# A two-layer retention and RG-LRU trunk on one core: every engine in the order of the program, weights split in two parts, first squares, softplus and final scaling regrouped

## The chip, the cores and the metric

The kernel runs on one core of one Trainium2 chip. The metric is the device time of one execution in microseconds (us); of the kernel before there are three runs, and their median counts.

## What is computed

The input x has 256 tokens of 2048 features, in float32. Two layers follow each other, and in each

- h = rmsnorm(x) g1, and one projection p = h w_in of width 6144, split into q, k, v, g of 1024 each (eight retention heads of 128) and xb, yb of 1024 each (the recurrent branch);
- retention per head: q and k are rotated, the scores are multiplied by a decay matrix, the weighted v is normalised over the head (mean and variance) and multiplied by silu(g);
- the recurrent branch: a causal convolution of 4 taps over xb, two gates (small block-diagonal products), a = exp(-8 r softplus(-lambda)), a linear recurrence over the tokens (a scan), times gelu(yb), and an rmsnorm over the branch;
- x = x + [retention, recurrent] w_out, then the feed-forward x = x + (silu(h w_gate) * (h w_up)) w_down with h = rmsnorm(x) g2 and 5632 inner features.

A last rmsnorm with its own gain gives the output. All products are made in float32 quality: an operand is the exact sum of two parts, and three of the four products of parts are taken.

## The kernel before, in words

Features lie on the 128 partitions and tokens along the free axis, so x is 16 chunks of [128 x 256]. A weight of 128 output features and up to 2048 inputs is one unit (a slot of 1 MB). For each unit SP loads `raw` (`load`, L533, three buffers), ACT copies it to its high part `whi` (L557), DVE subtracts to get the low part `wlo` (L558), and PE makes 16 pairs of products: the high weight with both parts of the operand (512 columns, L193) and the low weight with the high operand (256 columns, L195). Four pairs are a block, four blocks a unit. The first eight units of a layer make v with the roles exchanged (L438 to L440: three products of 512 columns per piece and half of the tokens, 24 in a unit). `split(n + 2, part)` (L549) runs while unit n is multiplied, in three parts, in front of blocks 0, 1 and 2; behind the last part the load of unit n + 5 is issued. The first four units of layer 0 come in quarters, together with quarters of x; `pair` (L122) makes the two parts of an operand: ACT the high (L126, L129), DVE the low (L127, L130).

Everything small follows the stream of blocks by a count of ticks, one for each block (`Ticks`, L51): `tk.after(n, f)` writes the instructions of f n blocks later. The head's scores (L237) come 5 ticks after k is done, the decayed scores (DVE, L244) 1 tick later, the weighted product (PE, L251) 2 ticks after that, the moments (DVE and POOL, L261 to L265) 1, the normed head (DVE, L272) 2, its transposes (PE, L286) 2, the gated mix and its pair 1. The recurrent branch goes from the convolution (ACT L317, DVE L319) over the gates (PE, L328) to tanh, exp and square on ACT (L336 to L340), square roots (L353), the scan (DVE, L360) and the accumulated squares (ACT L169, DVE L170). `sums` (L136) makes the norm's columns on PE (L141) and the power on POOL (L145); `spread` (L148) makes a row of them on all partitions, with a diagonal made by DVE (L153) and a product with ones (L155). After the recurrent branch's norm, eight ticks in a row each write a mix (L393) and its pair.

The program's order is not the order of the queues: the scheduler of the tile framework orders the instructions of each engine when the program is closed, and gives out buffers.

At the start POOL squares and adds the 16 chunks of x (L607 to L611), the sums follow at tick 23, their row at tick 25, and `softplus` (L565, 30 small operations on DVE) is written at tick 29. Eight small products warm PE up (L592). At the end the last chunk's square goes through `sums` together with the accumulated ones, `spread` makes the row, ACT copies it (L636), and 16 scalings of one chunk each follow (12 on DVE, L642; 4 on POOL, L640), with a transfer after every two, from SP and ACT in turn (L643).

Of the kernel before, what the change touches and what calls it, by code (L numbers as in the profile page):

```python
# [16 lines left out]
P = 128  # L17
T = 256
# [10 lines left out]
WARM = 8  # L29
# [21 lines left out]
class Ticks:  # L51
    """Work that follows the stream of large products, some ticks behind."""
# [18 lines left out]
class Unit:  # L71
    """One slot of a weight: its source, its width, its products, what follows."""

    def __init__(self, src, width, blocks, done=None, begin=None):
        self.src, self.width, self.blocks = src, width, blocks
        self.done, self.begin = done, begin
        self.split_at = (0, 1, 2)
# [3 lines left out]
def trunk(ctx: ExitStack, tc, a, out):  # L81
    nc = tc.nc
    pool = lambda name, bufs, **k: ctx.enter_context(tc.tile_pool(name=name, bufs=bufs, **k))
# [20 lines left out]
    # ---- constants and parameters  # L104
# [31 lines left out]
    def sums(parts, n, key):  # L136
        """1 / sqrt(sum over partitions and parts / n + eps), a column for each half of the tokens."""
        ps = small()
        for j in range(2):
            for i, x in enumerate(parts):  # L140
                PE.matmul(ps[:, j : j + 1], lhsT=x[:, j * P : (j + 1) * P], rhs=ones[:, 0:1],  # L141
                          start=i == 0, stop=i == len(parts) - 1)
        rc = two_p.tile([P, 2], F32, tag="rc", name="rc")
        V.tensor_scalar(out=rc, in0=ps[:, 0:2], scalar1=1.0 / n, scalar2=EPS, op0=ALU.mult, op1=ALU.add)  # L144
# [27 lines left out]
    def joined_halves(ps):  # L172
        """The two halves of a sum of products, added."""
# [5 lines left out]
    def column_unit(src, n_k, operand, done, begin=None, order=None):  # L179
        """128 output features, all tokens: n_k pieces of the contraction."""  # L180
# [22 lines left out]
    # ---- retention  # L203
# [10 lines left out]
    def head(l, h):  # L214
        c = {}

        def g_done(ps):
            """2 silu(g) = g (1 + tanh(g / 2))"""
# [81 lines left out]
    # ---- recurrent branch  # L300
    def lru(l, n):
# [30 lines left out]
        def decays():  # L332
            """r, i = (1 + tanh(./2)) / 2;  log a = n4sp (1 + tanh);  1 - a^2 = -tanh(log a) (1 + a^2)"""
# [45 lines left out]
        def cubic():  # L379
            """2 gelu(y) = y (1 + tanh(GELU (y + 0.044715 y^3)))"""  # L380
# [20 lines left out]
    # ---- norms between the blocks  # L401
# [4 lines left out]
    def after_residual(k, nxt, gains):  # L406
        """Chunk k of the residual is new: its part of the next norm and operand."""
# [12 lines left out]
    def v_units(l):  # L420
        """All tokens of half of v, 4 pieces of the contraction to a slot."""
# [38 lines left out]
    def layer_units(l):  # L460
# [15 lines left out]
        # output projection; the last head is the last to be ready  # L476
        order = [0, 1, 2, 3, 4, 5, 6] + list(range(8, 16)) + [7]
        for n in range(KD):
# [7 lines left out]
            if n == 1:  # L486
# [4 lines left out]
                u.split_at = (4, 4, 4)  # L491
            res.append(u)

        # feed-forward
# [26 lines left out]

    def last(k):
        if k < KD - 1:
            accumulate("xa", X[:, k, :], k == 0)
        else:
# [23 lines left out]
    def split(n, part, parts=3):  # L549
# [15 lines left out]
    def softplus():  # L565
        """-4 softplus(-lam), with log1p(e) = 2 artanh(e / (2 + e))"""
        lam = par[:, i0 : i0 + nl]
        V.tensor_scalar(out=sp[0], in0=lam, scalar1=-1.0, scalar2=None, op0=ALU.mult)
        V.tensor_tensor(out=sp[1], in0=sp[0], in1=lam, op=ALU.max)
        S.activation(out=sp[1], in_=sp[1], func=AF.Exp, scale=-1.0)  # L570
        V.tensor_scalar(out=sp[2], in0=sp[1], scalar1=2.0, scalar2=None, op0=ALU.add)
        V.reciprocal(out=sp[2], in_=sp[2])
        V.tensor_tensor(out=sp[1], in0=sp[1], in1=sp[2], op=ALU.mult)
# [141 lines left out]
```

## Time and profile before

| | |
|---|---|
| median of three runs | 2266.14 us (2265.61 to 2266.22) |
| span of the profiled execution, first to last instruction | 2262.9 us |
| mean granted TensorE clock | 0.996 |
| PE busy | 2239.7 us (99%) |
| DVE busy | 1530.3 us (68%) |
| ACT busy | 1160.7 us (51%) |
| POOL busy | 85.3 us (4%) |
| read from memory | 418.77 MB, 186 GB/s over the span |

The span leaves out what lies before the first and after the last instruction of the program; no time of its own is given for the profiled execution beside the span, which is 3.2 us below the median of the runs. Busy time is the union of an engine's instructions; PE's matmuls are pipelined and their ends are modelled. A row of a wait names the engine and line that waited, and the one that ended the wait. The lines are those of the kernel before.

### The profile page before, as it was taken

What the parts mean: (1) busy time and instruction counts of PE and PEld (TensorE: products, weight loads), DVE (VectorE), ACT (ScalarE), POOL (GpSimd) and SP (SyncE); (2) the same over time, 40 slices, a digit from 0 to 9 for tenths busy, and PEclk for the clock granted to TensorE, in tenths of its full rate; (3) what the DMA queues carried; (4) which work ended last, traced back from release to release, by engine and by line L of the source; (5) the groups of instructions that cost most, each with busy time, mean ns of one, the idle gap of its engine ahead of it and who ended that gap; (6) DMA issues with size and microseconds to landing.
All of it is one profiled execution on the core that took longest, in us unless ns stands there. A gap on an engine that the chain in (4) does not pass through costs nothing.

```text
span 2262.9 us, 32580 instructions
## 1 busy us (share of the span) xinstructions
PE 2239.7 (99%) x12748; PEld 1949.9 (86%) x12748; DVE 1530.3 (68%) x2818; ACT 1160.7 (51%) x2040; POOL 85.3 (4%) x128
## 2 busy tenths in 40 slices
PE   8999999999999999999999999999999999999997
PEld 6888888888888888888888888888888888888886
DVE  8788877666566666666758889776665666566665
ACT  5666644555344543445546765455543455444553
POOL 4001110000000000000000101000000000000000
PEclk9999999999999999999999999999999999999999
DMA  7455455555555555555555554555555555555553
GB/s 254 176 177 197 179 177 186 187 192 192 188 189 189 192 185 198 186 189 184 191 200 179 180 192 168 180 186 188 195 184 194 187 190 192 185 196 186 189 182 114
DMA packets 63721, 422.96 MB, mean 187 GB/s; under 512 B 7376, under 2 KB 8016, under 8 KB 25168
## 3 DMA queue, kind: packets, MB, share of 16 engines
q1 hardware_dynamic: 61200, 414.60, 51.7%
q0 software_dynamic: 1792, 5.24, 0.8%
q8 instruction: 99, 1.62, 0.3%
q10 hardware_dynamic: 576, 1.05, 0.1%
q14 instruction: 54, 0.44, 0.1%
HBM read 418.77 MB, written 2.10 MB: 186 GB/s over the span
## 4 chain that ended last, share of the span: by engine, by line
PE 97%; DVE 1%; DMA 1%; issue 0%; POOL 0%; ACT 0%; SPq 0%; DVEq 0%; POOLq 0%
PE acc_ps L193 61%; PE acc_ps L195 31%; PE v_ps L439 1%; PE v_ps L438 1%; PE v_ps L440 1%; PE sm_ps L328 1%; DVE wlo L558 1%; DMA x<-in_x_dram 0%; PE sm_ps L237 0%; DVE op L130 0%; DMA raw<-in_w_v_dram 0%; PE sm_ps L155 0%; PE sm_ps L286 0%; DVE x L642 0%; PE sm_ps L238 0%
## 5 line engine op out<-in xcount | busy, mean ns | idle before, releaser
L193 PE MATMUL acc_ps<-op,whi 128*128 128x512 f32 x6016 | 2105.6, 396 | 0.0
L195 PE MATMUL acc_ps<-op,wlo 128*128 128x256 f32 x6016 | 1672.9, 278 | 0.0
L193 PEld LDWEIGHTS acc_ps<-op,whi 128*128 128x128 f32 x6016 | 1128.8, 188 | 263.3
L558 DVE TENSOR_TENSOR wlo<-raw,whi 128x683 fp32r<-128x683 f32 (+5 forms) x1204 | 1007.5, 851 | 458.4 <-ACT whi L557 457.4
L557 ACT ACTIVATE whi<-raw 128x683 fp32r<-128x683 f32 (+5 forms) x1204 | 860.8, 754 | 853.3 <-PE acc_ps L193 765.7
L195 PEld LDWEIGHTS acc_ps<-op,wlo 128*128 128x128 f32 x6016 | 1131.5, 188 | 0.7
L403 DVE TENSOR_TENSOR x<-acc_ps,x 128x256 f32<-128x256 f32 x128 | 54.3, 424 | 219.1 <-PE acc_ps L195 219.1
L176 DVE TENSOR_TENSOR z<-acc_ps,low 128x256 f32<-128x256 f32 x256 | 107.1, 419 | 2.2 <-ACT low L175 2.2
L175 ACT ACTIVATE low<-acc_ps 128x256 f32<-128x256 f32 x256 | 93.9, 367 | 9.2 <-PE acc_ps L195 9.2
L126 ACT ACTIVATE op<-mix 128x256 fp32r<-128x256 f32 x104 | 43.4, 417 | 71.9 <-DVE mix L507 68.9
L502 ACT ACTIVATE sg<-z 128x256 f32<-128x256 f32 x88 | 36.8, 418 | 67.5 <-DVE z L501 67.5
L145 POOL TENSOR_TENSOR rc<-rc,mhalf 128x2 f32<-128x2 f32 x7 | 7.7, 1096 | 1684.8 <-DVE rc L144 1684.8
L439 PE MATMUL v_ps<-wlo,op 128*128 128x512 f32 x128 | 52.3, 409 | 7.5 <-DVE wlo L558 7.5
L404 DVE TENSOR_TENSOR x<-acc_ps,x 128x256 f32<-128x256 f32 x128 | 54.3, 424 | 4.3
L438 PE MATMUL v_ps<-whi,op 128*128 128x512 f32 x128 | 51.6, 407 | 1.2 <-ACT op L129 1.2
L440 PE MATMUL v_ps<-whi,op 128*128 128x512 f32 x128 | 51.7, 404 | 0.1
L127 DVE TENSOR_TENSOR op<-mix,op 128x256 fp32r<-128x256 f32 x104 | 43.5, 419 | 0.2
L439 PEld LDWEIGHTS v_ps<-wlo,op 128*128 128x128 f32 x128 | 25.3, 197 | 15.0 <-DVE wlo L558 10.1
L506 DVE TENSOR_TENSOR sg<-sg,rs 128x256 f32<-128x256 f32 x88 | 36.9, 420 | 0.8 <-ACT sg L502 0.8
L507 DVE TENSOR_TENSOR mix<-z,sg 128x256 f32<-128x256 f32 x88 | 36.9, 419 | 0.0
L501 DVE TENSOR_TENSOR z<-z,rs 128x256 f32<-128x256 f32 x88 | 36.9, 419 | 0.0
L130 DVE SCALAR_TENSOR_TENSOR op<-x,par,op 128x256 fp32r<-128x256 f32 x64 | 34.3, 539 | 0.2 <-ACT op L129 0.2
(114 smaller groups left out, 729.5 us busy)
## 6 DMA issues: line engine op xcount, KB each, us to landing
raw<-in_w_gate_dram SPq DMA_DIRECT2D x88, 1024.0 KB, 4.8
raw<-in_w_up_dram SPq DMA_DIRECT2D x88, 1024.0 KB, 4.8
raw<-in_w_in_dram SPq DMA_DIRECT2D x80, 1024.0 KB, 4.8
raw<-in_w_down_dram SPq DMA_DIRECT2D x64, 960.0 KB, 4.7
raw<-in_w_out_dram SPq DMA_DIRECT2D x32, 1024.0 KB, 4.8
raw<-in_w_down_dram SPq DMA_DIRECT2D x32, 896.0 KB, 4.5
raw<-in_w_v_dram SPq DMA_DIRECT2D x12, 1024.0 KB, 4.7
raw<-in_w_v_dram SPq DMA_DIRECT2D x16, 256.0 KB, 6.5
```

Of the source, the lines that this page charges most:

```text
L127: V.tensor_tensor(out=t[:, 1, :], in0=x_ap, in1=t[:, 0, :].bitcast(F32), op=ALU.subtract)
L175: S.activation(out=low, in_=ps[:, T : 2 * T], func=AF.Copy)
L176: V.tensor_tensor(out=z, in0=ps[:, 0:T], in1=low, op=ALU.add)
L193: PE.matmul(u.ps, lhsT=u.hi[:, w], rhs=x2.rearrange("p a t -> p (a t)"), start=k == order[0], stop=False)
L195: PE.matmul(u.ps[:, T : 2 * T], lhsT=u.lo[:, w], rhs=x2[:, 0, :], start=False, stop=k == order[-1])
L403: V.tensor_tensor(out=X[:, k, :], in0=ps[:, T : 2 * T], in1=X[:, k, :], op=ALU.add)
L404: V.tensor_tensor(out=X[:, k, :], in0=ps[:, 0:T], in1=X[:, k, :], op=ALU.add)
L438: PE.matmul(ps, lhsT=x2[:, 0, t], rhs=u.hi[:, w], start=k == 0, stop=False)
L439: PE.matmul(ps, lhsT=x2[:, 0, t], rhs=u.lo[:, w], start=False, stop=False)
L440: PE.matmul(ps, lhsT=x2[:, 1, t], rhs=u.hi[:, w], start=False, stop=k == KD - 1)
L557: S.activation(out=u.hi[:, w], in_=u.raw[:, w], func=AF.Copy)
L558: V.tensor_tensor(out=u.lo[:, w], in0=u.raw[:, w], in1=u.hi[:, w].bitcast(F32), op=ALU.subtract)
```

## The change

All engines take their instructions in the order in which the program writes them. A weight is split in two parts (of up to 1024 columns), in front of blocks 0 and 2. Twelve products warm up in place of eight. The first squares are made by ACT, four chunks at a time, at ticks 14 to 17, into a tile of the tag that v takes later (one buffer), and folded by DVE one tick later into a tile with two rows of tokens; the sums come at tick 20 and their row at tick 22. Softplus is written in six pieces at ticks 29 to 34. `spread` takes the column itself, broadcast, as the stationary operand and the identity as the moving one. Before the end the accumulated squares are summed early, the last chunk's square is added to them, and the scalings are four on DVE with three chunks each and four on POOL, with four transfers of four chunks.

```diff
-WARM = 8
+WARM = 12
 class Unit:
-        self.split_at = (0, 1, 2)
+        self.split_at = (0, 2)
 def trunk(ctx: ExitStack, tc, a, out):
     nc = tc.nc
+    ctx.enter_context(tc.manual_schedule())
...
     def sums(parts, n, key):
...
+        inverse_root([ps[:, 0:2]], n, key)
+
+    def inverse_root(columns, n, key):
         rc = two_p.tile([P, 2], F32, tag="rc", name="rc")
-        V.tensor_scalar(out=rc, in0=ps[:, 0:2], scalar1=1.0 / n, scalar2=EPS, op0=ALU.mult, op1=ALU.add)
+        w = 2 // len(columns)
+        for j, c in enumerate(columns):
+            V.tensor_scalar(out=rc[:, j * w : (j + 1) * w], in0=c, scalar1=1.0 / n, scalar2=EPS, op0=ALU.mult, op1=ALU.add)
         G.tensor_tensor(out=rc, in0=rc, in1=mhalf, op=ALU.pow)
...
     def spread(key):
-        dg = one_p.tile([P, 2, P], F32, tag="dg", name="dg")
         ps = small()
         for j in range(2):
-            V.tensor_scalar(out=dg[:, j, :], in0=ident, scalar1=st[key + "c"][:, j : j + 1], scalar2=None, op0=ALU.mult)
-        for j in range(2):
-            PE.matmul(ps[:, j * P : (j + 1) * P], lhsT=ones, rhs=dg[:, j, :], start=True, stop=True)
+            PE.matmul(ps[:, j * P : (j + 1) * P], lhsT=st[key + "c"][:, j : j + 1].to_broadcast([P, P]), rhs=ident,
+                      start=True, stop=True)
...
+    def last_sums():
+        st["last_ps"] = [small(), small()]
+        for j in range(2):
+            PE.matmul(st["last_ps"][j][:, 0:1], lhsT=st["xa"][:, j * P : (j + 1) * P], rhs=ones[:, 0:1], start=True, stop=False)
     def last(k):
         if k < KD - 1:
             accumulate("xa", X[:, k, :], k == 0)
+            if k == KD - 2:
+                tk.after(3, last_sums)
...
-    def split(n, part, parts=3):
+    def split(n, part, parts=2):
...
-    xa = one_p.tile([P, T], F32, tag="acc", name="acc")
-    G.tensor_tensor(out=xa, in0=X[:, 0, :], in1=X[:, 0, :], op=ALU.mult)
-    for k in range(1, KD):
-        sq = tmp("sq")
-        G.tensor_tensor(out=sq, in0=X[:, k, :], in1=X[:, k, :], op=ALU.mult)
-        G.tensor_tensor(out=xa, in0=xa, in1=sq, op=ALU.add)
-    tk.after(23, lambda: sums([xa], D, "rs"))
-    tk.after(25, lambda: rows("rs"))
-    tk.after(29, softplus)
+    def squares(i):
+        sq = one_p.tile([P, 4, T], F32, tag="v", name="sq4")
+        S.activation(out=sq, in_=X[:, 4 * i : 4 * i + 4, :], func=AF.Square)
+        tk.after(1, lambda: folded(i, sq))
+    def folded(i, sq):
+        if i == 0:
+            st["xa2"] = one_p.tile([P, 2, T], F32, tag="rotl", name="acc2")
+            V.tensor_tensor(out=st["xa2"], in0=sq[:, 0:2, :], in1=sq[:, 2:4, :], op=ALU.add)
+        else:
+            V.tensor_tensor(out=sq[:, 0:2, :], in0=sq[:, 0:2, :], in1=sq[:, 2:4, :], op=ALU.add)
+            V.tensor_tensor(out=st["xa2"], in0=st["xa2"], in1=sq[:, 0:2, :], op=ALU.add)
+    for i in range(4):
+        tk.after(14 + i, lambda i=i: squares(i))
+    tk.after(20, lambda: sums([st["xa2"][:, 0, :], st["xa2"][:, 1, :]], D, "rs"))
+    tk.after(22, lambda: rows("rs"))
+    for i, part in enumerate(softplus()):
+        tk.after(29 + i, part)
...
-                for part in range(3):
+                for part in range(2):
...
-    sums([st["xa"], st["sq"]], D, "rs")
+    for j in range(2):
+        PE.matmul(st["last_ps"][j][:, 0:1], lhsT=st["sq"][:, j * P : (j + 1) * P], rhs=ones[:, 0:1], start=False, stop=True)
+    inverse_root([ps[:, 0:1] for ps in st["last_ps"]], D, "rs")
...
-    for k in range(0, KD, 2):
-        for j in (k, k + 1):
-            if j % 4 == 3:
-                G.tensor_tensor(out=X[:, j, :], in0=X[:, j, :], in1=rs, op=ALU.mult)
-            else:
-                V.tensor_tensor(out=X[:, j, :], in0=X[:, j, :], in1=ps, op=ALU.mult)
-        (nc.sync if k % 4 == 0 else S).dma_start(out=out[:, k : k + 2], in_=X[:, k : k + 2, :])
+    row = ps.unsqueeze(1)
+    for k, n, pool_n, queue in ((0, 3, 1, nc.sync), (4, 3, 1, S), (8, 3, 1, nc.sync), (12, 3, 1, S)):
+        V.tensor_tensor(out=X[:, k : k + n, :], in0=X[:, k : k + n, :], in1=row.to_broadcast([P, n, T]), op=ALU.mult)
+        G.tensor_tensor(out=X[:, k + n, :], in0=X[:, k + n, :], in1=rs, op=ALU.mult)
+        queue.dma_start(out=out[:, k : k + 4], in_=X[:, k : k + 4, :])
```

The six pieces of softplus hold the same operations as before (the two scalings of the gates' biases move into the first piece).

## Rows read from the trace of the kernel before

**Rows 1.** The page: span, and busy time of each engine.

```profile
span 2262.9 us, 32580 instructions
PE 2239.7 (99%) x12748; PEld 1949.9 (86%) x12748; DVE 1530.3 (68%) x2818; ACT 1160.7 (51%) x2040; POOL 85.3 (4%) x128
```

**Rows 2.** Waits of PE, whole execution: us in total, times, longest us.

```profile
PE v_ps L439 <- DVE wlo L558: 7.5, 6, 3.8
PE sm_ps L286 <- DVE on L272: 1.4, 2, 0.7
...
PE v_ps L438 <- ACT op L129: 1.2, 1, 1.2
```

**Rows 3.** Stretches: us, busy PE, PEld, DVE, ACT, POOL, then PEclk, DMA share, GB/s.

```profile
0.00:40.00 40.00, 30.07 (x104) 22.61 (x105) 35.03 (x66) 19.86 (x39) 27.44 (x40) 0.91 0.68 231
160.00:270.00 110.00, 110.00 (x635) 95.93 (x634) 94.77 (x200) 73.69 (x131) 11.18 (x18) 1.00 0.52 183
270.00:300.00 30.00, 29.28 (x173) 25.52 (x172) 28.00 (x62) 16.62 (x32) 3.08 (x4) 1.00 0.47 169
400.00:1130.00 730.00, 730.00 (x4215) 638.51 (x4214) 456.24 (x797) 349.80 (x614) 1.25 (x1) 1.00 0.54 189
```

**Rows 4.** Groups of DVE and ACT from 160 to 270 us: busy us, mean ns, idle before.

```profile
L558 DVE TENSOR_TENSOR wlo<-raw,whi 128x683 fp32r<-128x683 f32 (+1 forms) x54 | 46.4, 864 | 8.6 <-ACT whi L557 8.4
L557 ACT ACTIVATE whi<-raw 128x683 fp32r<-128x683 f32 (+1 forms) x54 | 39.9, 768 | 19.0 <-PE acc_ps L193 19.0
...
L353 ACT ACT_TABLE_LOAD x5 | 6.4, 1283 | 0.1
...
L169 ACT ACTIVATE sq<-y 128x256 f32<-128x256 f32 x6 | 2.5, 410 | 4.1 <-DVE y L362 4.1
...
L317 ACT ACTIVATE xc<-xb,par 128x256 f32<-128x256 f32 x4 | 2.4, 603 | 3.1 <-DVE xb L314 3.1
...
L384 ACT ACTIVATE y<-y 128x256 f32<-128x256 f32 x4 | 1.7, 417 | 2.7 <-DVE y L383 2.6
```

**Rows 5.** Timelines of DVE and ACT near 271 us: start us, us, instruction.

```profile
271.01 0.87 DVE L393 SCALAR_TENSOR_TENSOR mix<-y,par,rs 128x256 f32<-128x256 f32 x2
271.97 0.43 DVE L127 TENSOR_TENSOR op<-mix,op 128x256 fp32r<-128x256 f32 x1
...
271.52 0.42 ACT L126 ACTIVATE op<-mix 128x256 fp32r<-128x256 f32 x1 [1.36 <-DVE mix L393]
```

**Rows 6.** Waits of DVE, whole execution: us in total, times, longest us.

```profile
DVE on L272 <- POOL ve L265: 12.3, 16, 0.9
DVE y L389 <- ACT y L384: 6.0, 10, 0.8
```

**Rows 7.** The start: groups (first 40 us), two stretches, PE's longest wait.

```profile
L592 PE MATMUL sm_ps<-ones 128*128 128x128 f32 x16 | 3.8, 431 | 1.0 <-DVE sp L575 1.0
...
L558 DVE TENSOR_TENSOR wlo<-raw,whi 128x512 fp32r<-128x512 f32 x16 | 14.7, 941 | 3.3 <-ACT whi L557 3.3
...
L578 DVE TENSOR_SCALAR sp<-sp 128x16 f32<-128x16 f32 x8 | 4.7, 588 | 0.1
...
10.50:17.20 6.70, 4.43 (x17) 2.71 (x15) 6.49 (x13) 4.89 (x11) 6.07 (x9) 1.00 1.00 367
17.40:24.00 6.60, 4.53 (x11) 3.58 (x12) 6.60 (x9) 6.38 (x14) 6.05 (x8) 0.50 0.78 292
...
19.48 0.80 PE L439 MATMUL v_ps<-wlo,op 128*128 128x512 f32 x1 [3.83 <-DVE wlo L558]
```

**Rows 8.** The chain of waits near the first sums: start us, us, what.

```profile
51.49 0.23 PE v_ps L440
51.71 0.34 PE sm_ps L141 x4
```

**Rows 9.** The end, timeline of DVE: start us, us, instruction.

```profile
2252.47 0.48 DVE L153 TENSOR_SCALAR dg<-ident,rc 128x128 f32<-128x128 f32 x2 [0.80 <-POOL rc L145]
2254.17 4.07 DVE L642 TENSOR_TENSOR x<-x,sm_ps 128x256 f32<-128x256 f32 x12 [1.22 <-ACT rs L636]
```

More of the change, by code (lines that the diff above doesn't have):

```diff
@@ L490, in layer_units @@
                 u.blocks.insert(3, held)
-                u.split_at = (4, 4, 4)
+                u.split_at = (4, 4)
             res.append(u)
@@ L567, in softplus @@
         lam = par[:, i0 : i0 + nl]
[L568 to L573, printed above, removed]
-        V.tensor_tensor(out=sp[2], in0=sp[1], in1=sp[1], op=ALU.mult)
@@ L575, in softplus @@
-        V.memset(sp[3], 1.0 / 17.0)
-        for j in range(15, 0, -2):
-            V.tensor_tensor(out=sp[3], in0=sp[3], in1=sp[2], op=ALU.mult)
-            V.tensor_scalar(out=sp[3], in0=sp[3], scalar1=1.0 / j, scalar2=None, op0=ALU.add)
-        V.tensor_tensor(out=sp[3], in0=sp[3], in1=sp[1], op=ALU.mult)
-        V.tensor_scalar(out=sp[0], in0=sp[0], scalar1=0.0, scalar2=None, op0=ALU.max)
-        V.scalar_tensor_tensor(out=sp[3], in0=sp[3], scalar=2.0, in1=sp[0], op0=ALU.mult, op1=ALU.add)
@@ L582, in softplus, with first @@
-        V.tensor_scalar(out=n4sp, in0=sp[3], scalar1=-4.0, scalar2=None, op0=ALU.mult)
-        for j, name in enumerate(("ba", "bx")):
-            b0 = PARAMS[name][0]
-            V.tensor_scalar(out=hb[:, j, :], in0=par[:, b0 : b0 + nl], scalar1=0.5, scalar2=None, op0=ALU.mult)
+        def first():
+            V.tensor_scalar(out=sp[0], in0=lam, scalar1=-1.0, scalar2=None, op0=ALU.mult)
+            V.tensor_tensor(out=sp[1], in0=sp[0], in1=lam, op=ALU.max)
+            S.activation(out=sp[1], in_=sp[1], func=AF.Exp, scale=-1.0)
+            V.memset(sp[3], 1.0 / 17.0)
+            for j, name in enumerate(("ba", "bx")):
+                b0 = PARAMS[name][0]
+                V.tensor_scalar(out=hb[:, j, :], in0=par[:, b0 : b0 + nl], scalar1=0.5, scalar2=None, op0=ALU.mult)
@@ new lines, in second, with terms @@
+        def second():
+            V.tensor_scalar(out=sp[2], in0=sp[1], scalar1=2.0, scalar2=None, op0=ALU.add)
+            V.reciprocal(out=sp[2], in_=sp[2])
+            V.tensor_tensor(out=sp[1], in0=sp[1], in1=sp[2], op=ALU.mult)
+            V.tensor_tensor(out=sp[2], in0=sp[1], in1=sp[1], op=ALU.mult)
+        def terms(js):
+            for j in js:
+                V.tensor_tensor(out=sp[3], in0=sp[3], in1=sp[2], op=ALU.mult)
+                V.tensor_scalar(out=sp[3], in0=sp[3], scalar1=1.0 / j, scalar2=None, op0=ALU.add)
@@ new lines, in end @@
+        def end():
+            V.tensor_tensor(out=sp[3], in0=sp[3], in1=sp[1], op=ALU.mult)
+            V.tensor_scalar(out=sp[0], in0=sp[0], scalar1=0.0, scalar2=None, op0=ALU.max)
+            V.scalar_tensor_tensor(out=sp[3], in0=sp[3], scalar=2.0, in1=sp[0], op0=ALU.mult, op1=ALU.add)
+            V.tensor_scalar(out=n4sp, in0=sp[3], scalar1=-4.0, scalar2=None, op0=ALU.mult)
+        return [first, second, lambda: terms((15, 13, 11)), lambda: terms((9, 7, 5)), lambda: terms((3, 1)), end]
```

## The prediction, made before the changed kernel ran

> **What bounds the kernel now.** I read the page's totals first: PE is busy for 2239.7 of a span of 2262.9 us [rows 1]. The runs have a median of 2266.14 us, 3.2 us above that span, and I carry these 3.2 us along unchanged: every sum below is a difference made in the span and added to 2266.1. A busy PE proves little, so the waits of PE came next. They are few: 7.5 us on weight parts (wlo) in the first stretch, two waits of 0.7 us on a normed head (L286), 1.2 us before the first product [rows 2]. The table by stretches then shows where something could change: the first 40 us (PE busy 30.07, clock 0.91), the projections (PE full, DVE 94.77 of 110), the end of a layer's projections (DVE 28.00 of 30) and the feed-forward stretch (DVE 456 of 730) [rows 3]. So there is little to win: about 10 us in the first 40, 1.4 at L286, and something behind the last product. And there is one place with little cover: the projections, where DVE has 15 us of 110 free.
>
> **The change part by part.**
>
> *Written order.* PE's order hardly moves: counted against the large products, its small ones already stand where the program puts them, the recurrent branch's sums alone come nine products later. DVE's does. In the present trace DVE does two mixes (L393) in a row, and the low part of the first (L127) only later, while ACT makes the high part (L126) in between [rows 5]. In written order the low part stands right behind its mix, and DVE stands idle until ACT has answered. I price such a round trip: ACT's operation (0.41 for a square or a copy, 0.42 for a tanh, 0.60 for the convolution's first step [rows 4]), a hop of about 0.04 each way (L126 ends at 271.94 and L127 starts at 271.97 [rows 5]), so 0.50, and 0.68 for the convolution. The nearest measured wait of this kind is L389 on L384, 6.0 us in 10 waits, 0.6 each [rows 6]; the bounds are 0 (ACT was ahead) and 0.8 (its longest). In the 110 us from 160 there are 4 convolutions, 4 tanh of the gelu, 6 squares, and 3 each of the gate's tanh and of the head's operand pairs: 16 x 0.50 + 4 x 0.68 = 10.7 us.
>
> A second wait hangs on it. ACT in written order does the next half of a weight only behind the operation of the round trip, and DVE wants that half's low part at once. A half is now 1024 columns. ACT's 683 took 0.768 [rows 4]; for 1024 I take 1.05, between 0.77 (no cost for columns) and 1.15 (in proportion). DVE returns from its own follow-up of 0.42 and waits another 1.05 + 0.04 - 0.42 = 0.67; where the low part stands directly behind (after the gelu's first square) it waits 0.42 + 1.05 + 0.08 = 1.55. Of the first kind I count 13 in the 110 us, of the second 4: 14.9, against 0 if ACT ran ahead. As ACT is sometimes ahead I take 12. The waits on POOL for the heads' norm (0.8 each, three) remain, 2.5 [rows 6], and the scans wait for square roots behind a table load of 1.28 [rows 4]: two pairs at 1.28 + 0.42 and the hops, 3.7 with some of it shared.
>
> *Two parts per weight.* 54 subtractions of 683 columns at 0.864 (46.7 us) become 36 of 1024 [rows 4]. I take 1.23 each, between 0.864 and 1.30 (in proportion): 44.3, a gain of 2.4 us of DVE in 110. The DMA of the next weight is issued behind the last part, at the third block as before, so SP's queue loses nothing.
>
> *The sum for the projections.* DVE would want 94.8 - 2.4 + 10.7 + 12 + 2.5 + 3.7 = 121 us of each 110, with the waits at 0 only 92. It falls behind by 11 us per 110; the stretch from the first head (about 95 us) to 270 us gives 175/110 x 11 = 17. In 270 to 300 it wants 28.0 - 0.6 plus 8 operand pairs at 0.50 plus 10 halves at up to 0.67: 38, another 8. That is 25 us per layer. PE follows, because the small products stand in its queue only two blocks (2.8 us) behind what DVE must have made for them: the weighted product (L251) behind the decayed scores (L244), the recurrent branch's sums (L141) behind its last square, the transposes (L286) behind the normed head. What DVE is late beyond 2.8 us becomes a wait of PE there; queued behind each are the large products of the next block. Two layers: 50 us, less the 1.4 that L286 waits already: **+48**. The bounds are -1.4 (no wait) and about +70 (every price at its upper end). I take a value near the upper middle because the measured wait is 0.6 and not 0.
>
> *Feed-forward and output projection.* Round trips occur there too (one pair and one silu in two units), but DVE is busy only 456 of 730 us [rows 3]; 44 pairs x 2 trips x 0.5 plus a half each behind them stay inside the 274 us that are free. Cost 0.
>
> *The first squares.* POOL's squares fill most of its 27.44 busy us in the first 40 [rows 3], and DVE's 512-column subtraction took 0.941 there although the larger 683-column one takes 0.864 elsewhere [rows 4, 7]; softplus put another 4.7 us of small operations (x8 at 0.588) and as much again of others between the weights. Both go, so DVE follows the weights, and the stall of 3.83 us at 19.48 should go with them, and with it the stretch of half clock behind it (granted 0.50 from 17.4 to 24.0, 11 products there against 17 before it, which themselves held waits) [rows 7]. But the new squares use one buffer: square i+1 on ACT waits until the sum of square i on DVE has freed it. And the sixth weight (slot 5, whose first half now stands before slot 4's second in ACT's queue) lands at an estimated 29 us: 8.9 MB of weights, x and tables take 24 to 30 us at the 367 and 292 GB/s of [rows 7], the first byte comes at 2 to 3. From there I add in written order: its high part 1.05, first square 1.05, high part of slot 4's second half 1.0, then on DVE three low parts and a sum (2 x 1.15 + 0.6 remaining), three times square and two sums (1.05 + 1.4), and between them slot 6's first half (2.3): some 15.5 us, so the squares are summed at about 44.5. PE has done 120 products by 36 and waits there about 8 us at the new sums (tick 20). Then 0.7 of sums and 18 products of 0.23 bring it to 49.5 at the point where it now stands at 51.71 [rows 8]; at half clock behind that wait, to about 53. Gain between 2.2 and -1.3; I take 1. Softplus, in six pieces, then lies in units of 5.5 us that hold 2.5 us of DVE's weight work, and costs 0; without that cover it would delay the same weights by up to 8 us. Four more warm-up products: eight took 3.8 us and were followed by a wait of 1.2 [rows 2, 7], so +0.7 at most, 0 taken.
>
> *The end.* Half of the last sums is done beforehand (4 passes, 0.34 [rows 8]), the diagonal (0.48) goes, and twelve scalings in 4.07 become four of 768 columns [rows 9], between 3.6 and 5.0. The four transfers of 0.5 MB replace eight; the last is 0.26 MB larger, 0.7 us at 367 GB/s. Bounds -1.5 and +1, taken -0.5.
>
> Sum: 2266.1 + 48 - 1 - 0.5 = 2312.6, say **2313 us**.
>
> **The clock.** In this trace PE waited 3.83 us and then ran at a granted 0.50 (1.2 GHz) until 24.0 [rows 7]. Whether each of the new waits does that is not in my sum: while DVE is the late one, a slower PE is hidden. The Trainium skill (TensorE: Matmul & The Clock Gate, section on HAM oscillation) says that idle gaps of a few microseconds put the array back to half rate, each time. By that rule the sum would be about 2330. The one stall of this trace agrees with it.
>
> **The rivals.**
> 1. *DVE becomes the bound in the projections*: the forecast, 2313, from 2290 to 2325 with its prices. For it: 86% busy there, and the order in [rows 5]. Chance 0.58.
> 2. *The same, and the clock falls after each long wait.* I expect four waits over 3.4 us in a layer (the two of L251 that follow a pair of scans, the branch's sums, the last transposes). A stretch of 6.6 us held 11 products where 29 of 0.23 fit; full of products at half clock it loses at most 3.3 us. Eight of these are 26, of which DVE's lateness hides about a third: 2313 + 17 = 2330. Chance 0.17.
> 3. *Faster: ACT keeps ahead, and the projections stay PE's.* The place is DVE's queue from 95 to 300 us in each layer; the point is 17.6 us of waiting per 110 us (15.2 free now, 2.4 saved by two parts), where the forecast has 28.9. Below it no wait reaches PE: then only -1.4 at L286, -1 to -8 in the first 50 us (the upper end if the square chain hides), -0.5 at the end: 2256 to 2263, say 2259. For it: ACT is busy only 73.69 of 110 [rows 3]. Against: the round trips are in the code and each needs ACT in turn. Chance 0.17.
> 4. *The order does not change*, because the present order on ACT and DVE is already nearly the written one: then start and end alone, 2264. Against: [rows 5]. Chance 0.08.
>
> **How the numbers follow.** About 0.2% (4.5 us) is what a measurement of this kernel can tell from no change. Slower: rivals 1 and 2, 0.75. Faster: rival 3, 0.17. Same: rival 4, 0.08. The likeliest time is 2313; the range of the slower cases alone is 2288 to 2336. To hold 8 in 10 the range goes down over the case of no change, to 2262, and leaves rival 3 out.
>
> **What would show it.** Right: PE waits at L251, L141 and L286 of 20 us or more in each layer; DVE near 100% in the projections with idle time put down to ACT's L557 and to the round trips; the feed-forward stretch unchanged; a wait of several microseconds at the first sums. Wrong: a PE without waits between 60 and 300 us, or a DVE whose share there falls below 90% without being waited for; then rival 3 stands. Eight stretches of half clock would mean rival 2.

## The result, and the profile after

The changed kernel takes 2349.74 us (median of four runs, 2336.07 to 2363.45), the kernel before 2265.9 beside it: a ratio of 1.037, interval 1.0329 to 1.041. It is slower by 84 us; the forecast was 47 slower, with a range that ended at 2336. The profiled execution is the shortest of the four, 2336.07 us, 70 above before. The page's totals, which answer to [rows 1]:

```profile
span 2334.3 us, 31734 instructions
PE 2257.4 (97%) x12760; PEld 1967.7 (84%) x12760; DVE 1565.6 (67%) x2408; ACT 1108.2 (47%) x1632; POOL 54.6 (2%) x97
```

PE's waits over the whole execution [rows 2]: us in total, times, longest.

```profile
PE sm_ps L255 <- DVE sT L248: 22.0, 8, 4.6
PE sm_ps L142 <- DVE acc L174: 14.9, 2, 7.5
PE sm_ps L290 <- DVE on L276: 12.1, 6, 4.6
PE sm_ps L142 <- DVE acc L640: 8.2, 1, 8.2
PE sm_ps L241 <- DVE kT L215: 4.1, 2, 2.0
```

The three products named in the prediction (now L255, L142 and L290) and the first sums (L142 behind L640) head the list. By stretches (us, busy PE, PEld, DVE, ACT, POOL, then PEclk, DMA share, GB/s), which answer to [rows 3]:

```profile
0.00:40.00 40.00, 32.54 (x144) 26.45 (x144) 24.50 (x42) 25.15 (x42) 0.69 (x6) 0.98 0.83 298
160.00:270.00 110.00, 101.57 (x563) 88.48 (x562) 86.31 (x159) 59.82 (x97) 6.60 (x14) 0.95 0.47 162
270.00:300.00 30.00, 22.49 (x118) 19.13 (x118) 21.38 (x40) 14.38 (x25) 2.33 (x4) 0.89 0.33 113
400.00:1130.00 730.00, 730.00 (x4216) 638.42 (x4215) 469.82 (x655) 338.15 (x477) 1.60 (x1) 1.00 0.54 189
```

In the 110 us from 160 PE made 563 products where it had made 635; in the feed-forward stretch 4216 for 4215. All of the profiled loss is in the two sections of projections. Comparing the same points of the two traces: the last product of v in layer 0 is 0.9 us later than before, the first residual 37.1, the start of layer 1 35.7, the end of its output projection 71.4, the last instruction 71.3.

What ended DVE's idle time from 160 to 270 us:

```profile
DVE wlo L570 <- ACT whi L569: 10.7, 13, 1.4
DVE xc L323 <- ACT xc L321: 3.0, 4, 0.8
DVE z L180 <- ACT low L179: 2.5, 5, 1.0
DVE acc L174 <- ACT sq L173: 2.1, 4, 0.5
DVE op L131 <- ACT op L130: 1.7, 3, 0.7
DVE sg L227 <- ACT sg L226: 1.3, 2, 0.8
DVE y L393 <- ACT y L388: 1.0, 2, 0.5
DVE on L276 <- POOL ve L269: 0.9, 1, 0.9
```

and the groups of the weight halves there [rows 4]:

```profile
L570 DVE TENSOR_TENSOR wlo<-raw,whi 128x1024 fp32r<-128x1024 f32 x33 | 39.8, 1220 | 10.7 <-ACT whi L569 10.7
...
L569 ACT ACTIVATE whi<-raw 128x1024 fp32r<-128x1024 f32 x32 | 32.9, 1047 | 0.0
```

One of PE's waits in full, as the timelines of DVE and PE have it (start us, us, instruction, idle before):

```profile
174.71 0.42 DVE L174 TENSOR_TENSOR acc<-acc,sq 128x256 f32<-128x256 f32 x1 [0.48 <-ACT sq L173]
...
177.20 0.43 DVE L174 TENSOR_TENSOR acc<-acc,sq 128x256 f32<-128x256 f32 x1 [0.55 <-ACT sq L173]
178.15 1.23 DVE L570 TENSOR_TENSOR wlo<-raw,whi 128x1024 fp32r<-128x1024 f32 x1 [0.52 <-ACT whi L569]
...
180.92 1.52 DVE L323 SCALAR_TENSOR_TENSOR xc<-xb,par,xc 128x256 f32<-128x256 f32 x3 [0.75 <-ACT xc L321]
182.36 1.22 DVE L570 TENSOR_TENSOR wlo<-raw,whi 128x1024 fp32r<-128x1024 f32 x1
183.50 0.55 DVE L248 TENSOR_TENSOR sT<-sm_ps,dec 128x384 f32<-128x384 f32 x1
...
184.10 0.79 PE L255 MATMUL sm_ps<-v,sT 128*128 128x128 f32 x2 [4.59 <-DVE sT L248]
```

Two scans' squares, two weight halves and a convolution stand in DVE's queue ahead of the decayed scores (L248), and before four of them DVE stands idle for ACT. PE stands at L255 for 4.59 us with the next block behind it.

The clock, in stretches that begin within such waits or at their end (PEclk is the third figure from the right):

```profile
38.20:51.90 13.70, 7.67 (x24) 6.51 (x25) 6.34 (x8) 3.74 (x4) 2.95 (x4) 0.50 0.39 141
181.60:188.40 6.80, 4.30 (x15) 3.91 (x16) 5.30 (x8) 3.74 (x6) 0.00 (x0) 0.50 0.59 216
232.80:236.20 3.40, 3.40 (x13) 3.06 (x13) 2.58 (x5) 1.58 (x4) 0.00 (x0) 0.50 0.38 89
287.40:294.20 6.80, 4.08 (x14) 3.62 (x15) 3.26 (x7) 1.65 (x4) 0.71 (x1) 0.50 0.19 48
321.50:324.90 3.40, 3.40 (x12) 2.85 (x11) 3.24 (x7) 0.04 (x1) 0.00 (x0) 0.51 0.87 308
1290.90:1294.30 3.40, 3.40 (x12) 2.83 (x12) 3.37 (x6) 0.80 (x2) 0.00 (x0) 0.50 0.70 241
```

In layer 0's projections the granted clock stood at 1.2 GHz in the last part of or behind the waits of 4.6, 3.8, 7.5 and 4.6 us, and not behind the waits of 2.0 us and less. Layer 1 differs: the last row begins 0.2 us behind the same wait of 2.04 us at L241 that brought no half clock in layer 0. So no length of wait that brings it can be read from here. The sections of both layers hold nine such stretches. The loss per layer, worked out from the starts of PE's products between the end of v and the first residual (292.9 us in layer 0 against 256.6 before, 293.4 against 256.6 in layer 1):

| us more than before | layer 0 | layer 1 |
|---|---|---|
| PE's waits | 26.8 | 24.8 |
| large products at half clock | 5.7 | 7.5 |
| small products, mostly at half clock | 3.4 | 3.7 |
| rest | 0.4 | 0.8 |

### The profile page after: what moved, and what is told of

Its sections match the earlier page's. It is cut to its first block, busy times and chain, and to the rows that moved or that the text cites. A ratio compares the mean times of both kernels' runs of the same rounds, so it can differ in the third digit from the quotient of the medians.

```text
span 2334.3 us, 31734 instructions
## 1 busy us (share of the span) xinstructions
PE 2257.4 (97%) x12760; PEld 1967.7 (84%) x12760; DVE 1565.6 (67%) x2408; ACT 1108.2 (47%) x1632; POOL 54.6 (2%) x97
## 3 DMA queue, kind: packets, MB, share of 16 engines
q10 hardware_dynamic: 288, 1.05, 0.1%
## 4 chain that ended last, share of the span: by engine, by line
PE 82%; DVE 10%; ACT 5%; issue 1%; DMA 1%; POOL 1%; DVEq 0%; SPq 0%; ACTq 0%
PE acc_ps L197 52%; PE acc_ps L199 26%; DVE wlo L570 4%; ACT whi L569 2%; PE v_ps L442 1%; PE v_ps L443 1%; PE v_ps L444 1%; DVE z L180 1%; DMA raw<-in_w_v_dram 1%; DVE lr L364 0%; DVE ru L214 0%; DVE rt L212 0%; DVE ru L213 0%; DVE on L276 0%; DVE y L366 0%
## 5 line engine op out<-in xcount | busy, mean ns | idle before, releaser
L570 DVE TENSOR_TENSOR wlo<-raw,whi 128x1024 fp32r<-128x1024 f32 (+3 forms) x808 | 933.7, 1190 | 304.4 <-ACT whi L569 300.8
L569 ACT ACTIVATE whi<-raw 128x1024 fp32r<-128x1024 f32 (+3 forms) x808 | 792.2, 1021 | 232.2 <-PE acc_ps L197 188.1
L173 ACT ACTIVATE sq<-x 128x256 f32<-128x256 f32 x59 | 24.7, 419 | 143.9 <-DVE x L408 143.9
L174 DVE TENSOR_TENSOR acc<-acc,sq 128x256 f32<-128x256 f32 x73 | 31.1, 425 | 38.3 <-ACT sq L173 38.3
```

What stands on the lines that cost most here:

```text
L569: S.activation(out=u.hi[:, w], in_=u.raw[:, w], func=AF.Copy)
L570: V.tensor_tensor(out=u.lo[:, w], in0=u.raw[:, w], in1=u.hi[:, w].bitcast(F32), op=ALU.subtract)
```

## The experiments

All kernels below are the changed one unless said otherwise, with the edit shown; times are medians.

### Written order or the other edits

```diff
-    ctx.enter_context(tc.manual_schedule())
```

> The changed kernel with the one line taken out that puts every engine in written order; all other edits stay. Theory A (in written order DVE stands idle in round trips to ACT, is late in the projections, and PE waits for it at the weighted product, the branch's sums and the transposes): the 71 us between sc0 and the end of both layers' projections go; 2258 to 2268 us, PE waits under 5 us in the projections of both layers together. Theory B (the cause is the weights in two parts of 1024 columns, which keep ACT and DVE too long on one instruction): the waits stay, over 2310 us.

Measured 2275.76 us (2268.23 to 2277.49), ratio 1.0033 [1.0021, 1.0044]. The waits in the projections are gone, and the trace is 10.5 us ahead of before from the end of v to the first residual. Then it loses 13 us in layer 0's feed-forward and 11 in layer 1's, without a wait of PE and at full clock. That was new, and is taken up below. The converse, the kernel before with that one line:

> The kernel before with that one line added, nothing else: three parts, squares on POOL, softplus in one piece. Theory A: the same waits in the projections, 60 to 90 us in the two layers, and some more at the start, where softplus now stands in one piece: 2335 to 2365 us. Theory B: no more than a few us, under 2285.

Measured 2353.0 us (2343.7 to 2373.7), ratio 1.0396 [1.034, 1.0452], with the same waits of PE:

```profile
PE sm_ps L252 <- DVE sT L245: 27.8, 8, 5.9
PE sm_ps L142 <- DVE acc L171: 17.2, 2, 8.7
PE sm_ps L287 <- DVE on L273: 8.0, 2, 4.0
```

So the written order alone carries the loss, in three parts as in two.

### Which engine's order

```diff
-    ctx.enter_context(tc.manual_schedule())
+    ctx.enter_context(tc.manual_schedule(engines={mybir.EngineType.DVE}))
```

> The changed kernel with DVE alone in written order; ACT, PE, POOL and SP are ordered by the scheduler. Theory A in its plain form (DVE's idle round trips are enough): half or more of the loss stays, 2300 to 2350 us. If ACT's order is what counts (its next half of a weight stands behind the operation of a round trip), most of the loss goes: 2262 to 2290 us.

2289.92 us (2280.06 to 2296.35), ratio 1.0109 [1.0072, 1.0146]. PE, POOL and SP in written order:

> The changed kernel with only PE, POOL and SP in written order; ACT and DVE are ordered by the scheduler. Theory A: like the kernel without the line, within 5 us of it, 2258 to 2270, since PE's order was nearly the written one already. A rival C, that it is PE's, POOL's or SP's fixed order that makes PE wait: over 2300 us.

2289.3 us (2284.92 to 2294.98), ratio 1.0104 [1.0082, 1.0126]; and ACT:

> The changed kernel with only ACT in written order; the other engines are ordered by the scheduler. With DVE alone in written order the projections cost some 15 us per layer, with all engines 36. Theory A (DVE's order is what makes it late): ACT alone costs less than 5 us per layer, 2265 to 2285 with the paces. Theory B (ACT behind a round trip holds back the next high part, so ACT's order costs by itself): 15 us or more per layer, 2295 to 2315, with PE waits of 15 us or more per layer. If both are additive, DVE's 15 and ACT's 20 make the 36.

2279.06 us (2278.26 to 2291.87), ratio 1.0074 [1.0048, 1.0101]. The projections between the end of v and the first residual took 256.6 us before and 292.9 after; here 273.8 with DVE's order, 261.3 with PE's, POOL's and SP's, 260.5 with ACT's. DVE's is the costliest, 17 of 36, just under the half that was expected of it, and the three together (17 + 5 + 4) stay 10 short of 36: the written orders cost more together than each by itself. The total times mislead here: DVE's stands at the upper end of the range that was meant for ACT's order, because the start gains 10 us in all three runs, and that of PE, POOL and SP is above its range, because in its profiled run both feed-forward stretches are slower with hardly a wait of PE, as in the run under the scheduler. Rival C, over 2300, falls. With DVE's order alone PE waits for the low parts, and hardly at L255:

```profile
PE acc_ps L199 <- DVE wlo L570: 10.8, 10, 2.6
PE sm_ps L290 <- DVE on L276: 3.1, 5, 0.7
PE sm_ps L255 <- DVE sT L248: 2.1, 3, 1.0
```

### The halves of a weight, and the distances

The low part one block behind the high part:

```diff
         S.activation(out=u.hi[:, w], in_=u.raw[:, w], func=AF.Copy)
-        V.tensor_tensor(out=u.lo[:, w], in0=u.raw[:, w], in1=u.hi[:, w].bitcast(F32), op=ALU.subtract)
-        if part == parts - 1:
-            load(n + RAW)
+        lows.append(low)
...
+                while lows:
+                    lows.pop(0)()
```

> The changed kernel, all engines in written order, but the low part of each half of a weight (DVE) is written one block behind its high part (ACT), the load of the next weight with it. By the prediction's sum the waits on halves are 12 of the 28.9 us that DVE waits in 110; without them 16.9 are left, below the 17.6 at which PE's waits begin. So theory A: the 36 us of a layer fall to under 8, 2270 to 2295 with the paces, and the half-clock stretches in the projections go with the waits. Rival, the other round trips (pairs, squares, tanh, root waits) carry the loss by themselves: 25 us or more per layer stay, 2320 or above.

2321.49 us (2320.34 to 2322.9), ratio 1.025 [1.0233, 1.0267]. PE's waits:

```profile
PE sm_ps L255 <- DVE sT L248: 17.8, 9, 4.1
PE sm_ps L142 <- DVE acc L174: 9.6, 2, 4.9
PE sm_ps L290 <- DVE on L276: 5.6, 2, 2.9
```

and DVE's from 160 to 270 us, where the wait on halves is nearly gone but another one has grown:

```profile
DVE z L180 <- ACT low L179: 6.6, 9, 1.4
...
DVE wlo L572 <- ACT whi L569: 1.6, 5, 0.5
```

The loss per layer falls from 36 us to 21.5 and 23.5, not below 8 as the prediction's threshold had it, and not staying at 25 or more as the rival had it. At z DVE waits for the unit to end on PE: it has caught up, and the time that it gains there cannot be used, because the next work in its queue isn't there yet. Longer distances instead:

```diff
-            tk.after(2, weighted)
+            tk.after(5 if h < NH - 2 else 2, weighted)
...
-            tk.after(2, normed)
+            tk.after(3 if h < NH - 2 else 2, normed)
...
-            tk.after(2, turned)
+            tk.after(4 if h < NH - 2 else 2, turned)
...
-                tk.after(2, lambda: sums([st["ya", l]], NL * P, "yr"))
+                tk.after(7, lambda: sums([st["ya", l]], NL * P, "yr"))
```

(the branch's row and mixes 5 ticks later with it).

> The changed kernel, all engines in written order, with more ticks between what DVE makes and the small product that reads it: for the heads 0 to 5 the weighted product 5 ticks behind the decayed scores (was 2), the normed head 3 (was 2), its transposes 4 (was 2); the sums of the recurrent branch 7 ticks behind its last scan (was 2), all that follows them 5 later. Theory A (bursts: DVE is behind by 2 to 7 us for a short time, and has caught up 8 us later): the waits at these products, 24 us per layer, fall to those of heads 6 and 7 and under 8 us, the half-clock stretches with them, the loss per layer from 36 to under 14, 2275 to 2310 with the paces. Theory B (throughput, the prediction's own: DVE wants more than it gets over the whole section): the waits only come later, 25 us or more per layer stay, 2325 or above.

2339.38 us (2330.86 to 2358.37), ratio 1.0336 [1.0294, 1.0378]. 33.5 us per layer stay, and the waits have moved to the scores:

```profile
PE sm_ps L241 <- DVE kT L215: 14.7, 6, 3.1
PE sm_ps L255 <- DVE sT L248: 14.0, 6, 3.4
PE sm_ps L290 <- DVE on L276: 13.2, 8, 3.4
```

This is theory B's outcome: with the waits on halves in place distance hardly helps. Both together, with the first sums at tick 24:

> Both cures in written order, the longer distances of the run before and the low part one block behind the high part, and the first sums at tick 24. Theory A: nearly no wait of PE is left in the projections (under 5 us per layer), the start is 4 to 10 us shorter than in the changed kernel, and the kernel runs between 2255 and 2290, where the pace of the feed-forward stretches (346.7 or 353.3 ns per pair, 13.9 us per layer) decides within that. Theory B: as for the low parts alone, 20 us per layer remain, 2310 to 2325.

2288.09 us (2287.62 to 2297.49), ratio 1.0107 [1.0092, 1.0123]. The start gains 9.7 us, 15.4 and 16.8 us per layer remain (11 of them waits). The total lies in theory A's range, the waits do not. Neither theory was right by its numbers: halves alone give back 14 us of 36, distance alone 3, both 20.

### The first sums

```diff
-    tk.after(20, lambda: sums([st["xa2"][:, 0, :], st["xa2"][:, 1, :]], D, "rs"))
-    tk.after(22, lambda: rows("rs"))
+    tk.after(24, lambda: sums([st["xa2"][:, 0, :], st["xa2"][:, 1, :]], D, "rs"))
+    tk.after(26, lambda: rows("rs"))
```

> The changed kernel with the first norm's sums at tick 24 and their row at tick 26, in place of 20 and 22. PE waited 8.2 us at these sums and then ran 13.65 us at half clock. Theory: both go, the scores of the first head come 8 to 11 us earlier than in the changed kernel, and the time is lower by that, at like paces 2325 to 2328 for the fastest run. Rival: DVE is behind anyway at that point, and the lost time comes back at the next wait: under 3 us.

2347.7 us (2346.11 to 2357.93), ratio 1.0373 [1.0351, 1.0396]. The wait falls from 8.2 to 3.3 us and the scores of the first head come 5.8 us earlier (90.2 for 96.0): between the two expectations, DVE is still late at tick 24. The total does not show it: in the profiled run the feed-forward stretch of layer 1 ran slower without a wait, which is taken up next.

### Two paces of the same products

> The changed kernel as it is, run again. Its four runs stood at 2336.1, 2349.3, 2350.2 and 2363.5 at a clock of 0.985 or 0.986 each, so neither the clock nor a disturbed run tells them apart. In the profiles PE's large pairs (a 512-column product and the 256-column one behind it) come every 346.7 us/1000 or every 353.3, without a wait, for a whole feed-forward stretch at a time. Theory of the two paces: some 2080 pairs of a layer from the output projection on at 6.67 ns more are 13.9 us, so the runs fall near 2336, 2350 and 2363, and a profile of a run at 2349 or above shows 353.3 ns in one feed-forward stretch or in both, with the waits of PE in the projections as before (52 us). Rival, waits of varying length: the runs lie anywhere between 2330 and 2370, and the profile's PE waits add up to more than 60 us where the run is longer.

2350.45 us (2349.09 to 2351.45), with the waits of the first profile to 0.7 us. Two profiles of one kernel, the same 710 us of feed-forward in layer 0, first the run of 2336.07 us, then one of 2349.09:

```profile
450.00:1160.00 710.00, 710.00 (x4098) 620.93 (x4097) 458.37 (x641) 327.56 (x463) 0.00 (x0) 1.00 0.55 190
```

```profile
450.00:1160.00 710.00, 710.00 (x4020) 616.25 (x4019) 448.40 (x624) 319.91 (x451) 0.00 (x0) 1.00 0.53 186
```

PE is busy without a gap and at full clock in both, and makes 78 products fewer in the second, 78 x 173.3 ns = 13.5 us. From the starts of the products: a pair (high and low) takes 346.7 ns in the one and 353.3 in the other, from the first pair of the stretch to the last. The runs of the changed kernel stand at these steps: 2336.1, six at 2349.1 to 2351.5, 2363.5, with none, one or two feed-forward stretches at the longer pace if a step is 13.5 us. The theory fits the two profiled runs, and for these the rival of varying waits falls; the run of 2363.5 was not profiled.

What sets the pace? The kernel before with one product of one column in every eighth unit of output projection and feed-forward (34 in all, their results unused):

```diff
+        if n % 200 >= 64 and n % 8 == 0:
+            PE.matmul(small()[:, 0:1], lhsT=ones, rhs=ones[:, 0:1], start=True, stop=True)
```

> The kernel before with one product of one column in every eighth unit of output projection and feed-forward (34 in all, 0.1 to 0.25 us each by the sums' products, so 4 to 8 us). Theory of the two paces: a short interruption is what can change the pace, so the stretches between two of them run at 346.7 or at 353.3 ns a pair with no other cause, and the time is 2266 + 4 to 8 + 6.67 ns for each pair at the longer pace, so anything from 2270 to 2300, with no wait of PE added. Rival, the pace comes from DVE's, ACT's or the DMA's work beside it: all pairs stay at 346.7 and the time is 2270 to 2274.

2301.16 us (2300.59 to 2301.41), ratio 1.0155 [1.014, 1.0171]: 35 us for 34 small products, just above the range expected. All stretches between them run at 353.3 ns; over 2096 pairs in each layer that is 28 us, and the 7 left are the products, 0.2 us each. Next, the change without written order and in three parts:

```diff
-    ctx.enter_context(tc.manual_schedule())
-        self.split_at = (0, 2)
+        self.split_at = (0, 1, 2)
```

> The changed kernel with the order left to the scheduler and weights in three parts as before, so that start, softplus, spread and end are all that is changed. Theory of the two paces: no waits of PE in the projections, the start 8 to 11 us shorter, 2254 to 2257 where both feed-forward stretches run at 346.7 ns a pair, 14 us more for each one that runs at 353.3. Rival, the two parts were what slowed the feed-forward stretches of the two-part kernel under the scheduler: then 2254 to 2257 in every run, and all stretches at 346.7.

2283.9 us (2283.63 to 2284.34), ratio 1.0079 [1.0067, 1.0092]: 10 us gained in the start, both feed-forward stretches at 353.3. In layer 0:

```profile
400.00:1130.00 730.00, 730.00 (x4134) 633.04 (x4133) 447.14 (x779) 342.90 (x601) 0.00 (x0) 1.00 0.52 185
```

The rival (two parts are to blame) falls. The same kernel with the row of a norm made as before, by a diagonal:

```diff
     def spread(key):
+        dg = one_p.tile([P, 2, P], F32, tag="dg", name="dg")
         ps = small()
         for j in range(2):
-            PE.matmul(ps[:, j * P : (j + 1) * P], lhsT=st[key + "c"][:, j : j + 1].to_broadcast([P, P]), rhs=ident,
-                      start=True, stop=True)
+            V.tensor_scalar(out=dg[:, j, :], in0=ident, scalar1=st[key + "c"][:, j : j + 1], scalar2=None, op0=ALU.mult)
+        for j in range(2):
+            PE.matmul(ps[:, j * P : (j + 1) * P], lhsT=ones, rhs=dg[:, j, :], start=True, stop=True)
```

> The scheduler's order, three parts, the changed start and end, but the row of the norm made as before, with the diagonal from DVE and a product with ones. In the kernel before the feed-forward stretch began at 346.7 ns a pair behind that product (the first large product behind it lasted 312 or 313 ns), in the run with the new product it began at 353.3 (316 ns). Theory of the two paces: the entry is as before, the stretches run at 346.7 and the start's 10 us are kept, 2254 to 2260, 14 more for each layer whose entry falls the other way. Rival, the longer pace comes from the start's or the end's edits by some lasting cause: 2280 or above again.

2254.82 us (2254.28 to 2254.84), ratio 0.9949 [0.9935, 0.9964]: 11 us faster than the kernel before, the start's 10 us kept. And the reverse, the kernel before with the new `spread` alone:

> The kernel before with one edit of the change alone: the row of a norm by a product of the broadcast column with the identity, without the diagonal. My forecast priced this at 0 (0.5 us less at the end). Theory of the two paces, with the entry set by this product: both feed-forward stretches at 353.3 ns a pair, 2 x 13.9 us more, 2290 to 2296, with no wait of PE added. Rival, the pace fell by chance in the runs of three parts: 2263 to 2267, or one layer of two, 2278 to 2281.

2294.77 us (2280.86 to 2294.97), ratio 1.0107 [1.0075, 1.0139]. The feed-forward stretch of layer 0, which held 4215 products before [rows 3], first in the kernel that is 11 us faster, then in the one before with the new product:

```profile
400.00:1130.00 730.00, 730.00 (x4207) 637.65 (x4207) 458.24 (x800) 349.82 (x614) 1.25 (x1) 1.00 0.54 189
```

```profile
400.00:1130.00 730.00, 730.00 (x4138) 633.14 (x4137) 445.05 (x775) 341.60 (x598) 1.25 (x1) 1.00 0.52 185
```

The edit is in three rows of each layer. The projections are 0.8 us longer with it; the row in front of the feed-forward, four short products in 0.4 us with either form, is followed by a stretch that is 14 us longer. The single run at 2280.86 is lower by the size of one layer's step. Over all profiles (without the one with 34 extra products) the ten feed-forward stretches behind a diagonal begin at the short pace, and 12 of the 26 behind the broadcast column. Two parts with the diagonal:

> The same with two parts per weight. If the pace is set at the entry and by what interrupts PE later (with two parts the run under the scheduler had interruptions of 0.1 us at the first units of the down projection), the time is 2254 to 2260 without, up to 2284 with a change of pace. If two parts cost DVE or ACT time that PE feels, waits of PE of 5 us or more are seen.

2272.03 us (2266.14 to 2274.39), ratio 1.0025 [1.0015, 1.0034], no wait of PE over 1.5 us. The stretches begin at 346.7 ns and change pace at the first units of the down projection, where two pairs in a row are late (522 and 456 ns from start to start in layer 0); layer 0 goes back to the short pace at a later such place. One stretch of the two-part run under the scheduler had changed at the same place. The row 5 ticks behind the chunk in place of 4 (the first gate unit is then still scaled by the earlier norm's row):

> Three parts, the scheduler's order, the new product for the row, but that row of the second norm written 5 ticks behind the chunk and not 4. Nothing of the work changes. Theory of the two paces: either 2283 to 2285 as without the shift, or a step of 14 or 28 us less, with no wait changed. Rival, the pace is a property of the program's work: 2283 to 2285.

2283.92 us (2283.78 to 2284.32): no step; the position alone did not change the pace. Last, the diagonal in written order:

> The changed kernel, all engines in written order, with the diagonal of before for the rows of the norms. Waits of PE and half clock in the projections stay: 71 us over before. If the entry by the diagonal leaves the short pace also behind waits, every run stands at 2334 to 2340; if the waits scatter the entry, runs spread over 2336, 2350 and 2364 as those of the changed kernel do.

2351.7 us (2342.61 to 2358.89), ratio 1.0376 [1.0343, 1.0409]. In the profiled run, 2346.13 us, PE also waits 6.5 us for the diagonal, and both feed-forward stretches run at 346.7 ns: the short pace is left behind waits too. It is 10 us above the shortest run of the changed kernel, 8 of them by its longer projections (297.7 and 296.8 us for 292.9 and 293.4). Two runs, 2357.27 and 2358.89, are some 12 us longer still, about a step; whether one of their stretches had the longer pace is not shown.

## Why the prediction was right and where it failed

**Written order makes DVE late: right.** The waits stand where they were put, and their size came out: 25 us per layer forecast, 26.8 and 24.8 measured. So were the prices: a half 1.220 for 1.23 on DVE, 1.047 for 1.05 on ACT; 12 for the waits on halves and 13.2 for round trips and POOL in 110 us of work, against 10.7 and 10.0 in the same window, in which 563 of 635 products were made (12.1 and 11.3 for the whole work). The 3.7 for square roots did not appear. PE's order, which "hardly moves", and ACT's had no price of their own: alone, PE's with POOL's and SP's costs 5 us per layer, ACT's 4.

**The rule that turned them into a loss: wrong, though its result held.** It set DVE's wants against its time in 110 us, with a threshold of 17.6. With the halves apart the 16.9 us of waits that the sum leaves should have been free, and 22 us per layer were lost. DVE's idle time in front of a unit's end (z, 6.6 us) can't be saved up for the burst behind the next scans. That the rule gave 25 where 26.8 and 24.8 were measured was thus in part luck.

**"Whether each of the new waits does that is not in my sum: while DVE is the late one, a slower PE is hidden": the first step that failed.** The clock fell at all waits of 3.8 us and more, and once behind one of 2.04; 9 us in layer 0 and 11 in layer 1 were not hidden: 20 us. Rival 2, with chance 0.17, had this mechanism at 17 us, and its sign, eight stretches of half clock, was met with nine. The Trainium skill (TensorE: Matmul & The Clock Gate, HAM oscillation) has idle gaps of a few microseconds put the array back to half rate each time; the trace agrees for the waits of 3.8 us and more, as in the row at 0.50 that begins in the 4.59 us wait, and not for every shorter one (2.04 us in layer 0). The 48 forecast for the waits and 20 for the clock make the 70 us of the profiled run within 2.

**"Feed-forward: cost 0": the second.** The reason given, DVE's free time, holds; PE is never waited for there. But the cost is that of PE's own pace: 13.5 us in the profiled run of 2349.09, close to the median, and none in the shortest. The trace before held both paces: its feed-forward stretches ran at 346.7 ns, the last 244 pairs of each output projection at 353.4. But nothing in it told which one a changed start of the stretch would give. Forecast 47, and 20 for the clock, and 14 for the pace are the 84 within 3.

**The start: the time right, the reason half.** Gain forecast 1, measured a loss of 0.9; the wait at the new sums was 8.2 us for 8, and half clock followed up to 51.9. What the edits at the start are worth, 10 us, shows in full where the scheduler orders ACT, DVE or both; in written order 4.9 of it with the first sums at tick 24, and 9.7 with the low parts a block later and longer distances besides. It is more than rival 3's 1 to 8.

**The end: right.** 0.5 us forecast, 0.6 measured between the last residual and the end. The four scalings took 3.54 us together, just below the forecast's 3.6 to 5.0:

```profile
2325.35 3.54 DVE L674 TENSOR_TENSOR x<-x,sm_ps 128x768 f32<-128x768 f32 x4 [1.99 <-ACT rs L671]
```

**The edit of `spread`, costed by its own work alone (half a microsecond less at the end)**, costs 29 us in the kernel before. **Two parts**, costed as a gain of DVE's time, show no gain of their own under the scheduler: with the diagonal they are slower (2272 against 2255), with the broadcast column faster (2276 against 2284), and both ways the feed-forward's pace accounts for most of it.

What stays open: why a pair has two paces at all, and why one row's products lead into the one and another's into the other. That the row in front changes the pace is shown by exchanging it, in the kernel before and in the changed one with three parts; how it does so is not. Which part of the written order outside DVE adds the last 10 us per layer is open too.

## What to carry to other kernels

An order written out by hand must keep an engine from waiting on its partner: write the follow-up of a round trip later than the round trip (for the weight halves that gave back 14 of 36 us per layer), and price every wait of PE together with the half clock behind it. Where a matrix stream is 100% busy, count products per microsecond: a busy share of 1.00 hid 2%. Such a stream's pace can depend on a small product in front of it, so measure each edit of that kind by itself, and look at the spread of the runs for steps of one size. Of this change the new start and end are worth keeping, with the scheduler's order, three parts and the diagonal: 2254.82 us.

## What the runs showed of the hardware

A stream of pairs (512 and 256 columns, each with its own weight load of 188 ns) has two steady paces, 346.7 and 353.3 ns, at the same granted clock of 2.4 GHz. In the short one successive starts repeat as, for instance, 231, 113, 232, 118 ns, in the long one as 236, 114, 232, 118, 240, 120. A pace holds until something interrupts the stream. A sign shows early: the distance from the start of the first large product behind the small ones to the next start. Of the 36 feed-forward stretches in the profiles (without the run with 34 extra products) those with 313 ns or less went on at the short pace in 13 of 14 cases, with 314 or 315 in 9 of 11, with 316 to 319 in none of 11. It is a sign and not shown to be the cause, and it holds for this place only: of the output projections' stretches behind a transposition 26 of 28 at 314 or 315 ran at the long pace. The two profiles of the changed kernel differ there by 3 ns (313 and 316, in front of layer 0's feed-forward) and by 13 us at the end. The Trainium skill (TensorE: Matmul & The Clock Gate, Back-to-back issue gap) says that in a stream of loads and products the spacing is set by both. Either pace here is longer than 325 ns, an estimate from the page's formula for the two products alone (216 and 109), which fits that; but the page also has 512 columns come down to about 131 ns in such a stream, and here they stand at 230 or more: the measurement decides.
